# Second attention with query halves stacked on the rows and two score products a head

## The chip, the cores and the metric

The kernel runs on one core of one Trainium2 chip. The metric is the device time of one execution in microseconds (us); lower is better. TensorE (PE) multiplies matrices into eight PSUM banks, VectorE (DVE) and ScalarE (ACT) work element by element, GpSimd (POOL) does the same more slowly, and SyncE (SP) issues the transfers.

## What is computed

Two blocks of a transformer over 512 positions of 1024 features, everything in float32. The first has two layers and is not touched. The second, cut to what matters here:

```python
proj = h @ w_in                       # u_glu, q, k, v, gate_logits
u = ua * jax.nn.sigmoid(ub)
u = conv31(u) + conv_b                # depthwise, 31 taps along time
u = jax.nn.silu(layer_norm(u, conv_ln_g, conv_ln_b))
y_conv = u @ conv_w_out + conv_b_out

q1, q2, k1, k2 = rope(...)            # 8 heads of 64 each; v: 8 heads of 128
a = softmax(q1 k1^T) - lam * softmax(q2 k2^T)     # causal, in blocks of 128 queries
y_att = rms_norm(a v, head_norm) * (1 - lam_init)

g_conv, g_att = jnp.split(jax.nn.sigmoid(gate_logits), 2, axis=-1)
y = (g_conv * y_conv + g_att * y_att) @ w_o
```

A feed-forward layer follows.

## The kernel before

A float32 product is made of three fast products: each operand is split in a high and a low part, and `mm3` (lines 459 to 464) adds high x high, high x low and low x high in one bank. Weights arrive in one stream of units of 128x1024. For each unit SP loads `raw`, ACT copies the high half to `wh` (line 377), DVE subtracts to get the low half `wl` (line 380). `raw`, `wh` and `wl` are rings of three. Units that are needed for long ("held") go into 128x512 slots instead. Line 380 is the helper behind all additions, subtractions and multiplications of two tensors, line 398 the one behind scalar-tensor-tensor operations, line 377 the one behind all ACT operations, line 544 the mask with its row minimum.

The second block (`second`, line 1357) begins with the two GLU inputs (1602 to about 1711 us in the trace). Then come four parts of the attention, two heads of v each: query/key projections of four units into four banks (`pq`), copied out by ACT and rotated by `rope2`; value projections (`pv`, held units); and, as `GATES` says, some of the 16 gate units, all of them behind part 3. Then eight units of `conv_w_out_2` follow, and eight of `w_o_2` (from 2066.10 us).

Beside these projections run two lanes of generators. `beat` counts the triples of products and calls `tick` at every third; each lane then takes as many steps as its rate has saved up. The lane "conv" is the depthwise convolution: 8 tiles of 30 taps, one DVE operation each (line 398, with `cw`), in groups of three. The lane "att" is the attention: `_diff_turn` transposes the rotated queries and keys (line 1663) and splits them; `_diff_block` does the scores of one block of queries (line 1691), mask (544), exponentials on ACT, the difference (398, with `dka`), transposes (1715), product with v (1723), the normalization (`dss`, with one POOL operation) and a transpose back (1741). A score tile needs 64 rows of contraction: two softmax halves lie in rows 0 to 63 and 64 to 127 of a tile, and each half has three products.

The building program may set instructions of different lanes in another order on an engine than they are written, but each engine then runs its list strictly in that order. Banks and slots come from lists of free ones, oldest first, so a projection may be given a bank that an attention step still holds.

Of the kernel before, what the change touches and what calls it, by code (L numbers as in the profile page):

```python
# [16 lines left out]
R1, R2, R3, R4, R5, R6 = 0.9, 1.0, 0.6, 0.6, 0.8, 1.5  # L17
# [8 lines left out]
GATES = (0, 0, 0, 16)  # L26
# [56 lines left out]
def _units_second():  # L83
# [4 lines left out]
    gates = [("w_in_2", 0, 0, 8, c + 128 * m, 128) for c in (6144, 5120) for m in range(8)]  # L88
# [43 lines left out]
HELD = {i for i, u in enumerate(UNITS) if _is_held(i, u)}  # L132

# [175 lines left out]
class Net:  # L309
# [90 lines left out]
    def split(self, hi, lo, src, scale=None):  # L400
# [17 lines left out]
    def _fetch(self, between=None):  # L418
# [3 lines left out]
        off, s = PIECES[i]  # L422
        raw = self.small("raw", (128, 1024), bufs=3)
# [8 lines left out]
        if i in HELD:  # L432
            wh, wl = [], []
            per = 512 // _cols(u)
            for k in range(0, u[3], per):
# [3 lines left out]
                self.split(h, l, raw[:, c].rearrange("p (k c) -> p k c", k=n))  # L439
# [3 lines left out]
        else:  # L443
            h = self.small("wh", (128, 1024), F32R, bufs=3)
            l = self.small("wl", (128, 1024), F32R, bufs=3)
            for c in parts:
                self.split(h[:, c], l[:, c], raw[:, c])
# [909 lines left out]
    def second(self, follow, out):  # L1357
# [6 lines left out]
        def convolve(i):  # L1364
            acc = self.big(f"acc{i}")
            self.act(acc, us[i], AF.Identity, scale=self.cw[:, 31 * i + 30:31 * i + 31], bias=self.p("conv_b", i))
            for j in range(29, -1, -1):
                s = 30 - j
                self.stt(acc[:, s:], us[i][:, :512 - s], self.cw[:, 31 * i + j:31 * i + j + 1], acc[:, s:], ALU.mult, ALU.add)
                if j % 3 == 0:  # L1370
                    yield
            self.free(us[i])
            conv.append(acc)
            if i == 1:
                csum.append(self.big("csum"))
                self.add(csum[0], conv[0], conv[1])
            elif i > 1:
                self.add(csum[0], csum[0], acc)

        csum, cn = [], []  # L1380
        cl = self.lane("conv", 1, R3)
        ths = {}
# [59 lines left out]
        self.lane("conv", 1, R4)  # L1442
        for part in range(4):
            pq = [self.psum(f"pq{t}") for t in range(NTB)]
# [11 lines left out]
            self.free(pq)  # L1456
            for t in range(NTB):
                self.rope2(ra[t], cos[:, t], sin[:, t])
# [18 lines left out]
            al.waiting += self.diff_attention(part, ra, vv, ya, done)  # L1477
            if part == 3:
                cl.waiting.append(self.conv_norm(conv, csum, cn))
                self.lane("conv", 1, R5)  # L1480
            for m in range(sum(GATES[:part]), sum(GATES[:part + 1])):
# [3 lines left out]
        self.lane("att", 2, R6)  # L1485
# [155 lines left out]
    def rope2(self, a, cos, sin):  # L1641
# [9 lines left out]
        self.add(a, a, b)  # L1651
        self.free(b)

    def diff_attention(self, part, ra, vv, ya, done):
        qk = []
        left = [NTB]
        return [self._diff_turn(ra, qk)] + [self._diff_block(part, n, qk, vv, ya, left, done) for n in range(NTB)]

    def _diff_turn(self, ra, qk):
        for j in range(4):  # L1660
            pt = self.psum("qkT", (128, 4, 128))
# [168 lines left out]
```

## Time and profile before

| | |
|---|---|
| median of 3 runs | 2490.43 us (2488.10 to 2490.53) |
| the profiled execution | 2488.26 us |
| its span | 2486.1 us |
| PE busy | 2444.6 us (98%) |
| DVE busy | 1638.6 us (66%) |
| ACT busy | 1064.8 us (43%) |
| POOL busy | 318.7 us (13%) |
| mean granted clock of PE | 0.994 |

The profile is one execution, and its span begins with the first instruction; the time of the execution is 2.2 us longer than the span. Busy times of PE overlap, since a product's last columns drain while the next one starts: the distance between two starts is what a product costs in a row. The granted clock is a share of 2.4 GHz; 0.5 is 1.2 GHz.

### The profile page before, as it was taken

The numbers are of one execution on the slowest core, as the hardware profiler recorded it, in microseconds if no ns is written. First come the engines' busy times: TensorE is split into PE (matmuls) and PEld (weight loads), VectorE is DVE, ScalarE is ACT, GpSimd is POOL, SyncE is SP. The second block draws the span as 40 slices with busy tenths as digits, with TensorE's granted clock in tenths as the row PEclk, the third lists the DMA queues.
The fourth block names the chain that finished last, engine by engine and source line by source line (L and its number), as shares of the span: only waits on it lengthen the run. The fifth ranks groups of instructions, "written<-read, shape, count | busy, mean of one in ns | idle before, by whom it ended". The sixth has DMA issues, their size and how long they took to land.

```text
span 2486.1 us, 32470 instructions
## 1 busy us (share of the span) xinstructions
PE 2444.6 (98%) x12206; PEld 2053.9 (83%) x12206; DVE 1638.6 (66%) x3064; ACT 1064.8 (43%) x1984; POOL 318.7 (13%) x820
## 2 busy tenths in 40 slices
PE   9999999999999999999999999999999989999998
PEld 7888888888888888888888788988887769988887
DVE  6998755444355488865677644799899675643335
ACT  6567433332234365643423223523445565634222
POOL 7923000000056054100000000000000000000000
PEclk9999999999999999999999999999999989999999
DMA  4222232222323322133466633322211113122232
GB/s 156 86 71 77 80 132 93 96 100 94 101 97 128 97 73 75 60 102 127 133 219 207 222 113 107 126 89 103 77 60 68 47 64 119 69 93 89 94 106 76
DMA packets 83677, 256.57 MB, mean 103 GB/s; under 512 B 9536, under 2 KB 10944, under 8 KB 83520
## 3 DMA queue, kind: packets, MB, share of 16 engines
q1 hardware_dynamic: 83520, 254.50, 30.2%
q8 instruction: 95, 1.56, 0.3%
q14 instruction: 62, 0.51, 0.1%
HBM read 248.18 MB, written 6.29 MB: 102 GB/s over the span
## 4 chain that ended last, share of the span: by engine, by line
PE 83%; DVE 7%; DMA 5%; ACT 2%; issue 2%; SPq 0%; POOL 0%; DVEq 0%; POOLq 0%; ACTq 0%
PE bank L462 26%; PE bank L463 26%; PE bank L464 26%; DMA slot<-in_wada_dram 4%; DVE slot L380 2%; DVE wl L380 2%; ACT slot L377 2%; DVE slot L398 2%; PE bank L1691 1%; PE bank L1723 1%; DMA raw<-in_w_dram 0%; PE bank L1194 0%; PE bank L1206 0%; DVE slot L394 0%; PE bank L1014 0%
## 5 line engine op out<-in xcount | busy, mean ns | idle before, releaser
L462 PE MATMUL bank<-slot,wh 128*128 128x512 f32 x2456 | 964.5, 394 | 7.3 <-ACT slot L377 7.3
L464 PE MATMUL bank<-slot,wl 128*128 128x512 f32 x2456 | 959.7, 392 | 2.8 <-DVE wl L380 2.8
L463 PE MATMUL bank<-slot,wh 128*128 128x512 f32 x2456 | 959.9, 391 | 0.0
L377 ACT ACTIVATE wh<-raw 128x1024 fp32r<-128x1024 f32 (+3 forms) x369 | 385.2, 1045 | 774.2 <-PE bank L463 401.8
L380 DVE TENSOR_TENSOR wl<-raw,wh 128x1024 fp32r<-128x1024 f32 (+3 forms) x369 | 450.4, 1221 | 216.9 <-ACT wh L377 214.9
L462 PEld LDWEIGHTS bank<-slot,wh 128*128 128x128 f32 x2456 | 463.5, 189 | 105.8 <-ACT slot L377 9.1
L464 PEld LDWEIGHTS bank<-slot,wl 128*128 128x128 f32 x2456 | 462.5, 188 | 102.8 <-DVE wl L380 6.0
L463 PEld LDWEIGHTS bank<-slot,wh 128*128 128x128 f32 x2456 | 463.2, 189 | 95.3 <-DVE slot L398 0.7
L380 DVE TENSOR_TENSOR slot<-bank,slot 128x512 f32<-128x512 f32 (+4 forms) x340 | 197.4, 592 | 229.3 <-PE bank L464 207.9
L377 ACT ACTIVATE slot<-slot 128x512 fp32r<-128x512 f32 (+4 forms) x378 | 207.6, 558 | 293.6 <-DVE slot L380 269.8
L380 DVE TENSOR_TENSOR slot<-slot,slot 128x512 f32<-128x512 f32 (+4 forms) x480 | 288.4, 619 | 50.2 <-ACT slot L377 47.1
L377 ACT ACTIVATE slot<-bank 128x512 f32<-128x512 f32 (+7 forms) x398 | 182.7, 475 | 128.2 <-PE bank L464 47.8
L463 PE MATMUL bank<-wl,slot 128*128 128x512 f32 (+1 forms) x480 | 180.9, 377 | 0.0
L464 PE MATMUL bank<-wh,slot 128*128 128x512 f32 (+1 forms) x480 | 180.1, 376 | 0.0
L462 PE MATMUL bank<-wh,slot 128*128 128x512 f32 (+1 forms) x480 | 179.5, 377 | 0.0
L463 PE MATMUL bank<-slot,slot 128*128 128x256 f32 (+1 forms) x624 | 178.3, 291 | 0.3 <-DVE slot L398 0.3
L464 PE MATMUL bank<-slot,slot 128*128 128x256 f32 (+1 forms) x624 | 178.3, 290 | 0.0
L398 DVE SCALAR_TENSOR_TENSOR slot<-slot,slot 128x512 f32<-128x512 f32 (+1 forms) x184 | 123.9, 689 | 81.1 <-DMA slot<-in_wada_dram 58.0
L462 PE MATMUL bank<-slot,slot 128*128 128x256 f32 (+1 forms) x624 | 176.5, 292 | 0.3 <-ACT slot L377 0.3
L398 DVE SCALAR_TENSOR_TENSOR slot<-slot,cw,slot 128x485 f32<-128x485 f32 (+28 forms) x240 | 166.6, 731 | 1.9 <-ACT slot L377 1.1
L380 DVE TENSOR_TENSOR slot<-slot,bank 128x512 f32<-128x512 f32 (+1 forms) x104 | 66.2, 644 | 128.8 <-PE bank L464 128.5
L463 PEld LDWEIGHTS bank<-slot,slot 128*128 128x128 f32 x624 | 118.9, 192 | 2.6 <-DVE slot L398 0.5
(197 smaller groups left out, 2163.2 us busy)
## 6 DMA issues: line engine op xcount, KB each, us to landing
raw<-in_w_dram SPq DMA_DIRECT2D x373, 512.0 KB, 3.3
slot<-in_wada_dram SPq DMA_DIRECT2D x96, 256.0 KB, 5.0
raw<-in_w_dram SPq DMA_DIRECT2D x32, 448.0 KB, 3.4
slot<-in_x_dram SPq DMA_DIRECT2D x16, 256.0 KB, 3.8
xd<-slot SPq DMA_DIRECT2D x16, 256.0 KB, 3.8
slot<-xd SPq DMA_DIRECT2D x16, 256.0 KB, 3.6
out_dram<-slot SPq DMA_DIRECT2D x8, 256.0 KB, 2.0
slot<-in_bc_dram SPq DMA_DIRECT2D x8, 128.0 KB, 3.1
```

What stands on the lines that cost most here:

```text
L377: return self.nc.scalar.activation(out=out, in_=in_, func=func, scale=scale, **kw)
L380: return (eng or self.nc.vector).tensor_tensor(out=out, in0=a, in1=b, op=op)
L398: return self.nc.vector.scalar_tensor_tensor(out=out, in0=a, scalar=s, in1=b, op0=op0, op1=op1, **kw)
L462: t.matmul(ps, ah, bh, start=start, stop=False)
L463: t.matmul(ps, ah, bl, start=False, stop=False)
L464: t.matmul(ps, al, bh, start=False, stop=stop)
L1691: nc.tensor.matmul(ps[e][:, :w], qk[s][x][rows, tn], qk[2 + s][y][rows, :w], start=i == 0, stop=i == 2)
L1723: nc.tensor.matmul(po[:, e], at[e][:, b], vv[b // 2][:, b % 2, 128 * e:128 * e + 128], start=b == 0, stop=b == n)
```

## The change

The two score products. `_diff_turn` now lays the queries of one softmax half out twice on 128 rows, the high part in 64 rows and the low part in the other 64 (`qs`). Keys are copied twice side by side before their transposes (`kd`), so that a key tile has the same 64 rows twice, once as a high tile and once as a low one. One product of `qs` with the high keys and one with the low keys take the place of the three: 128 score products in place of 192. There are 32 more transposes (32 of queries and 64 of keys in place of 64). The doubling is an addition on POOL of the two rope terms, and DVE adds only the query half.

Weight halves. For the units of `w_in_2` behind the first six and for `conv_w_out_2` the low half is subtracted on POOL: 50 operations of 128x1024 and 16 of 128x512.

Gates, rates and yields. Parts 1 and 2 get two gates each and part 3 has twelve, in the order of `GATE_ORDER`. The attention lane runs at 1.65 steps a tick in place of 1.0, and the convolution lane at a rate worked out from the steps left. The accumulator of a convolution lies in a bank, and ACT copies it out at the end. `dfin` has three buffers. Some `yield`s move.

In all PE's list goes from 11,855 to 11,823 instructions, DVE's from 2,968 to 2,918, ACT's from 1,818 to 1,842 and POOL's from 825 to 907; up to the end of the GLU inputs PE's list is the same.

```diff
-R1, R2, R3, R4, R5, R6 = 0.9, 1.0, 0.6, 0.6, 0.8, 1.5
+R1, R2, R3 = 0.9, 1.65, 0.6
-GATES = (0, 0, 0, 16)
+GATES = (0, 2, 2, 12)
+GATE_ORDER = (0, 1, 2, 3, 4, 5, 8, 9, 10, 11, 12, 13, 14, 15, 6, 7)
+BESIDE = {i for i, u in enumerate(UNITS) if i >= _SECOND + GLU_HELD and u[0] in ("w_in_2", "conv_w_out_2")}
...
-            self.sub(lo, src, hi.bitcast(F32))
+            self.sub(lo, src, hi.bitcast(F32), eng)
...
+        eng = self.nc.gpsimd if i in BESIDE else None
...
-            acc = self.big(f"acc{i}")
+            acc = self.psum(f"acc{i}")
...
-            conv.append(acc)
+            conv.append(self.big(f"conv{i}"))
+            self.act(conv[i], acc)
...
+            self.free(acc)
...
+            cl.rate = steps[0] / (16 * (4 - part) + 8 / 3 * (6 - sum(GATES[:part])))
...
-            for m in range(sum(GATES[:part]), sum(GATES[:part + 1])):
+            for m in GATE_ORDER[sum(GATES[:part]):sum(GATES[:part + 1])]:
...
-        self.add(a, a, b)
+        self.add(a[:, 0:4], a[:, 0:4], b[:, 0:4])
+        k, kb = (z[:, 4:8].unsqueeze(2).to_broadcast([128, 4, 2, 64]) for z in (a, b))
+        self.add(kd, k, kb, self.nc.gpsimd)
...
+        for s in range(2):
+            pt = self.psum("qT", (128, 4, 128))
             for t in range(NTB):
+                self.nc.tensor.transpose(pt[:, t], ra[t][:, 2 * s:2 * s + 2].rearrange("p h d -> p (h d)"), self.ident)
+            src = pt.rearrange("p t d -> p (t d)")
+            qs = [self.big("qs", F32R) for _ in range(2)]
+            for e in range(2):
+                rows, rest = slice(64 * e, 64 * e + 64), slice(64 - 64 * e, 128 - 64 * e)
+                self.act(qs[e][rows], src[rows])
+                self.sub(qs[e][rest], src[rows], qs[e][rows].bitcast(F32))
             self.free(pt)
+            ks = []
+            for e in range(2):
+                yield
+                pt = self.psum("kT", (128, 4, 128))
+                for t in range(NTB):
+                    self.nc.tensor.transpose(pt[:, t], kd[t][:, 2 * s + e].rearrange("p i d -> p (i d)"), self.ident)
+                ks.append((self.big("kh", F32R), self.big("kl", F32R)))
+                self.split(*ks[e], pt.rearrange("p t d -> p (t d)"))
+                self.free(pt)
...
-            for i, (x, y) in enumerate(((0, 0), (0, 1), (1, 0))):
-                for e in range(2):
-                    rows = slice(64 * e, 64 * e + 64)
-                    nc.tensor.matmul(ps[e][:, :w], qk[s][x][rows, tn], qk[2 + s][y][rows, :w], start=i == 0, stop=i == 2)
+            for e in range(2):
+                for i in range(2):
+                    nc.tensor.matmul(ps[e][:, :w], qk[s][0][e][:, tn], qk[s][1][e][i][:, :w], start=i == 0, stop=i == 1)
...
+        self.lanes["conv"].rate = 0.7
```

The order on the engines, at the end of part 1's query/key projections. First PE before: L462 to L464 are the three products of `mm3`, L1691 the scores of one half.

```order
L462 MATMUL bank_64<-wh_152,slot_12627 128x512
L463 MATMUL bank_64<-wl_155,slot_12627 128x512
L464 MATMUL bank_64<-wh_152,slot_12628 128x512
L1691 MATMUL bank_70<-slot_13899,slot_13838 128x512
L1691 MATMUL bank_70<-slot_13900,slot_13838 128x512
L1691 MATMUL bank_70<-slot_13899,slot_13839 128x512
L462 MATMUL bank_63<-slot_14379,slot_12564 128x256
L463 MATMUL bank_63<-slot_14380,slot_12564 128x256
L464 MATMUL bank_63<-slot_14379,slot_12565 128x256
```

Three products of a score stand between the last triple of the query/key projections and the first of the value projections (128x256).

The same place on PE after: the last 13 instructions of a stretch of 28 that has no projection, and the gate's projection that ends it. L1720 is the new score product, L1744 the transposes of the difference, L1752 the product with v, L1770 the transpose back, L469 and L470 the new lines of `mm3`; x2 stands for two that read alike.

```order
L1720 MATMUL bank_63<-slot_13887,slot_13857 128x512
L1720 MATMUL bank_68<-slot_13964,slot_13911 128x512
L1720 MATMUL bank_68<-slot_13965,slot_13911 128x512
L1744 MATMUL bank_64<-cst,slot_14038 128x128 x2
L1770 MATMUL bank_66<-cst,slot_14197 128x128 x2
L1720 MATMUL bank_69<-slot_13944,slot_13910 128x384
L1720 MATMUL bank_69<-slot_13945,slot_13910 128x384
L1744 MATMUL bank_70<-cst,slot_14040 128x128 x2
L1752 MATMUL bank_64<-slot_13786,slot_14108 128x128 x2
L469 MATMUL bank_63<-slot_12564,wh_152 128x512
L470 MATMUL bank_63<-slot_12565,wh_152 128x512
```

The projection that follows writes bank_63, in which a score of 512 columns has just been put; it can start when the mask has read that.

DVE after, at the end of the 53 instructions that stand beside this stretch: L404 with `cw` is a tap of the convolution (now into bank_67), L404 with `dka` the difference of the two halves, L551 the mask and its row minimum.

```order
L404 SCALAR_TENSOR_TENSOR bank_67<-slot_13234,cw_11510,bank_67 128x489
L404 SCALAR_TENSOR_TENSOR dka_14035<-dsm_14033,nlam_11506,dri_14034 128x2
L400 TENSOR_SCALAR drs_14037<-dri_14034 128x2
L404 SCALAR_TENSOR_TENSOR bank_67<-slot_13234,cw_11510,bank_67 128x488
L386 TENSOR_TENSOR dss_13971<-dss_13971,dfin_14126 128x2
L404 SCALAR_TENSOR_TENSOR slot_14038<-slot_14039,dka_14035,slot_14038 128x256
L404 SCALAR_TENSOR_TENSOR slot_14040<-slot_14041,dka_14035,slot_14040 128x256
L404 SCALAR_TENSOR_TENSOR bank_67<-slot_13234,cw_11510,bank_67 128x487
L551 ISA slot_14310,dmx_14043<-bank_63,slot_13534 128x512
L551 ISA dmx_14043 128x1
```

The mask that reads bank_63 is the last but one of the list; ahead of it stand taps, rope operations and the differences. At the ends of parts 2 and 3 PE's list has the like, with 33 and 25 instructions, ended by the value projections.

## Rows read from the trace of the kernel before

**Rows 1.** The page, part 1: busy time, share of span, instructions.
```profile
PE 2444.6 (98%) x12206; PEld 2053.9 (83%) x12206; DVE 1638.6 (66%) x3064; ACT 1064.8 (43%) x1984; POOL 318.7 (13%) x820
```
**Rows 2.** Windows: length, busy of PE, PEld, DVE, ACT, POOL; PE's clock; DMA.
```profile
1800.00:1820.00 20.00, 19.38 (x125) 17.16 (x125) 18.42 (x37) 8.16 (x20) 0.00 (x0) 1.00 0.04 15
...
1920.00:1940.00 20.00, 17.33 (x79) 12.84 (x77) 17.73 (x42) 9.29 (x26) 0.00 (x0) 0.91 0.16 53
...
1980.00:2000.00 20.00, 12.06 (x74) 9.07 (x72) 16.24 (x38) 17.38 (x41) 2.37 (x3) 0.83 0.01 2
2000.00:2020.00 20.00, 19.35 (x72) 15.17 (x73) 15.00 (x33) 11.33 (x28) 0.00 (x0) 0.83 0.37 128
...
2060.00:2080.00 20.00, 18.60 (x148) 17.40 (x147) 11.67 (x26) 12.90 (x33) 1.39 (x2) 1.00 0.32 114
```
**Rows 3.** Windows around the two dips of the granted clock.
```profile
1931.70:1935.10 3.40, 3.40 (x10) 2.63 (x9) 3.40 (x13) 1.70 (x6) 0.00 (x0) 0.50 0.00 0
1993.10:2006.80 13.70, 9.50 (x29) 7.20 (x30) 13.70 (x33) 13.70 (x32) 0.00 (x0) 0.50 0.06 16
```
**Rows 4.** Timeline of PE: start, length, instruction, [idle before <-releaser].
```profile
1989.40 0.60 PE L1663 MATMUL bank<-cst,slot 128*128 128x128 f32 x4
1989.96 0.33 PE L1691 MATMUL bank<-slot,slot 64*128 64x128 f32 x2
...
1994.64 0.90 PE L1691 MATMUL bank<-slot,slot 64*128 64x128 f32 x5 [2.74 <-DVE slot L380]
...
2000.65 0.80 PE L462 MATMUL bank<-slot,wh 128*128 128x512 f32 x1 [0.97 <-ACT slot L377]
```
**Rows 5.** Timeline of PE, two runs of score products and what follows them.
```profile
1837.12 0.94 PE L1691 MATMUL bank<-slot,slot 64*128 64x128 f32 x12
1837.99 0.38 PE L462 MATMUL bank<-slot,slot 128*128 128x256 f32 x1
...
1869.61 0.96 PE L1691 MATMUL bank<-slot,slot 64*128 64x512 f32 x3
1870.50 0.50 PE L462 MATMUL bank<-slot,wh 128*128 128x512 f32 x1
1870.84 0.40 PE L463 MATMUL bank<-slot,wh 128*128 128x512 f32 x1
1871.08 0.40 PE L464 MATMUL bank<-slot,wl 128*128 128x512 f32 x1
```
**Rows 6.** Groups of DVE, 1720 to 2070 us: busy us, mean ns | idle before.
```profile
L380 DVE TENSOR_TENSOR wl<-raw,wh 128x1024 fp32r<-128x1024 f32 x33 | 40.3, 1221 | 11.7 <-ACT wh L377 11.1 <-PE bank L464 0.6
L380 DVE TENSOR_TENSOR slot<-slot,slot 128x512 f32<-128x512 f32 x57 | 37.9, 687 | 0.3 <-ACT slot L377 0.2
...
L398 DVE SCALAR_TENSOR_TENSOR slot<-slot,slot,slot 128x512 f32<-128x512 f32 x16 | 11.4, 746 | 4.1 <-DMA slot<-xd 4.0
L544 DVE CUSTOM_DVE_ANT_0 slot<-bank,slot 128x512 f32<-128x512 f32 x16 | 10.9, 688 | 8.1 <-PE bank L1691 8.1
...
L380 DVE TENSOR_TENSOR slot<-slot,slot 128x256 f32<-128x256 f32 x24 | 9.2, 421 | 0.2 <-ACT slot L377 0.2
```
**Rows 7.** Groups of POOL over the whole span: busy us, mean ns | idle before.
```profile
L380 POOL TENSOR_TENSOR s_xx<-slot,s_steps 128x256 f32<-128x256 f32 x32 | 19.1, 618 | 0.5
...
L380 POOL TENSOR_TENSOR s_xx<-slot,s_steps 128x64 f32<-128x64 f32 x32 | 10.7, 354 | 0.5
```
**Rows 8.** Timeline of DVE and POOL in the first block.
```profile
916.88 0.73 POOL L380 TENSOR_TENSOR slot<-s_xx 128x256 f32<-128x256 f32 x1
916.89 0.74 DVE L380 TENSOR_TENSOR sm<-sm,es 128x4 f32<-128x4 f32 x1
...
917.67 0.48 DVE L544 CUSTOM_DVE_ANT_0 slot<-bank,cst,nsink 128x256 f32<-128x256 f32 x1
917.69 0.61 POOL L380 TENSOR_TENSOR s_xx<-slot,s_steps 128x256 f32<-128x256 f32 x1
```
**Rows 9.** Timeline of DVE: six operations in a row.
```profile
1988.59 4.06 DVE L398 SCALAR_TENSOR_TENSOR slot<-slot,slot,slot 128x512 f32<-128x512 f32 x6
```

More of the change, by code (lines that the diff above doesn't have):

```diff
@@ L87, in _units_second @@
         u.append(("w_in_2", 0, 0, 8, 128 * i, 128))
-    gates = [("w_in_2", 0, 0, 8, c + 128 * m, 128) for c in (6144, 5120) for m in range(8)]
+    gates = [("w_in_2", 0, 0, 8, (6144 if m < 8 else 5120) + 128 * (m % 8), 128) for m in GATE_ORDER]
     for part in range(4):
@@ L1456, in second @@
             self.free(pq)
+            kd = [self.big("kd", shape=(128, 4, 2, 64)) for _ in range(NTB)]
             for t in range(NTB):
-                self.rope2(ra[t], cos[:, t], sin[:, t])
+                self.rope2(ra[t], kd[t], cos[:, t], sin[:, t])
             wv = [self.unit("w_in_2") for _ in range(2)]
@@ L1476, in second @@
                 ya[m] = self.big(f"ya{m}")
-            al.waiting += self.diff_attention(part, ra, vv, ya, done)
+            al.waiting += self.diff_attention(part, ra, kd, vv, ya, done)
             if part == 3:
                 cl.waiting.append(self.conv_norm(conv, csum, cn))
-                self.lane("conv", 1, R5)
-            for m in range(sum(GATES[:part]), sum(GATES[:part + 1])):
+                cl.rate = steps[0] / 5
+            for m in GATE_ORDER[sum(GATES[:part]):sum(GATES[:part + 1])]:
                 gate(m)
@@ L1484, in second @@
         self.finish("conv")
-        self.lane("att", 2, R6)
         ys = []
@@ L1650, in rope2, with diff_attention, _diff_turn @@
         self.mul(a, a, tab(cos))
[L1651 removed]
+        self.add(a[:, 0:4], a[:, 0:4], b[:, 0:4])
+        k, kb = (z[:, 4:8].unsqueeze(2).to_broadcast([128, 4, 2, 64]) for z in (a, b))
+        self.add(kd, k, kb, self.nc.gpsimd)
         self.free(b)
[L1654 removed]
+    def diff_attention(self, part, ra, kd, vv, ya, done):
         qk = []
         left = [NTB]
[L1657 to L1661, printed above, removed]
+        return [self._diff_turn(ra, kd, qk)] + [self._diff_block(part, n, qk, vv, ya, left, done) for n in range(NTB)]
+    def _diff_turn(self, ra, kd, qk):
+        for s in range(2):
+            pt = self.psum("qT", (128, 4, 128))
             for t in range(NTB):
[L1663 to L1669 removed]
+                self.nc.tensor.transpose(pt[:, t], ra[t][:, 2 * s:2 * s + 2].rearrange("p h d -> p (h d)"), self.ident)
[5 more added lines that the diff above has]
+                self.sub(qs[e][rest], src[rows], qs[e][rows].bitcast(F32))
+            self.free(pt)
+            ks = []
[7 more added lines that the diff above has]
+                self.free(pt)
+            qk.append((qs, ks))
+            if s == 1:
+                self.free(ra, kd)
             yield
@@ L1673, in _diff_block @@
         nc = self.nc
-        while len(qk) < 4:
+        while len(qk) < 2:
             yield
@@ L1709, in _diff_block @@
         if n == NTB - 1:
-            self.free(qk)
+            self.free([[q, k] for q, k in qk])
         at = []
@@ L1726, in _diff_block @@
             self.free(at[e])
-            if e == 0:
-                yield
-        fin = self.small("dfin", (128, 2), bufs=2)
+        yield
+        fin = self.small("dfin", (128, 2), bufs=3)
         self.stt(fin, ss, HEAD_LIMIT, rs, ALU.is_lt, ALU.mult)
@@ L1732, in _diff_block @@
         self.powm(ss, ss, 2)
+        yield
         self.mul(ss, ss, fin)
```

22 lines of the change are left out of this document (9 added, 13 removed).

## The prediction, before the run

> **What bounds the kernel now.** I read the page first: TensorE (PE) is busy 98% of the span [rows 1], so the time is PE's own work plus the places where PE waits or runs at half clock. Next the windows of 20 us over the second attention: PE is full in nearly all of them. The idle time stands in five (20 less PE's busy time): 0.62 + 2.67 + 7.94 + 0.65 + 1.40 = 13.3 us [rows 2]. VectorE (DVE) is at 16 to 18 of 20 us in the first three of these. Two narrower windows show the granted clock at 0.50, that is 1.2 GHz, each behind a stretch in which PE waited [rows 3]. The first costs half of 3.4 us, 1.7. In the second PE has no projection until 2000.65 [rows 4]; from there to 2006.80 it loses half of 6.15, 3.1. So waits and clock take 13.3 + 4.8 = 18.1 us: all that a smoother second attention can give back.
>
> The largest of these stretches is the pattern to remember. From 1989.96 to 2000.65 PE's list holds score products alone, with no projection behind which a wait could hide, and it sits through 2.74 us waits for DVE [rows 4]. DVE meanwhile runs one queue of long vector operations.
>
> **The change part by part.**
>
> *Score products.* Before, each of the two softmax halves of a head has three products on 64 rows. Most of the time one half stands alone between projections: three of 512 columns take 1870.50 - 1869.61 = 0.89 us, and the first projection behind them 0.34 where the next takes 0.24, so 0.10 more [rows 5]. Twelve of 128 columns take 0.87, so three take 0.22 [rows 5]. I draw a line between these for 256 and 384 columns (0.44 and 0.67). Sixteen triples of each width are 16 x (0.22 + 0.44 + 0.67 + 0.89) = 35.5 us, and 52 separate runs, counted in the same view, pay the 0.10: 40.7 in all. After, there are 32 products of each width on 128 rows. One of 512 columns is priced as a projection of that size, 0.24; in proportion 0.18 and 0.12, and 0.11 for 128 columns: 32 x 0.65 = 20.8. That saves 19.9. The stacking adds 32 transposes; four take 1989.96 - 1989.40 = 0.56 [rows 4], so 32 x 0.14 = 4.5. Net on PE: -15.4. PE is the bound, so this is on the path.
>
> A rule speaks against this part. The Trainium skill ("TensorEngine Tiling (Array Packing)", Overview) says that products with a contraction of 64 rows can run side by side, up to twice as fast. If all pairs had, the old triples would have cost 17.8 + 5.2 = 23.0, and the gain would be 2.2 in place of 19.9. The rows bear this out only where both halves stand next to each other, as in the twelve of 0.87; a half that stands alone takes 0.30 for each product of 512 columns, more than the 0.24 of a full-height one.
>
> *Weight halves to GpSimd (POOL).* DVE loses subtractions of 1.22 us, 33 of them in 350 us [rows 6], so 40 us of about 300 busy ones. POOL gets them. A POOL operation of 64 columns takes 354 ns and of 256 columns 618 [rows 7], a slope of 1.38 ns a column: 1024 columns cost at least 0.62 + 768 x 0.00138 = 1.67 us. From a 256-column operation of 0.73 us [rows 8], four times that is 2.9. I take 2.2, and keep both ends. A unit of eight blocks is 24 projections of 0.24, so 5.8 us on PE; even 2.9 fits inside this, with two more units ready in the ring. Price on PE as long as DVE and POOL don't block each other: 0.
>
> *Doubled keys.* Half of the rope addition leaves DVE (512 columns at 687 ns become 256 at 421 [rows 6], 16 x 0.27 = 4.3 us less) and POOL gets 16 additions of 512 columns, at 0.97 to 1.46 by the same two rows; I take 1.2. Queued behind them on POOL are the next weight halves.
>
> *DVE and POOL together.* Here the trace warns. A DVE multiplication of 4 columns, both inputs in SBUF, took 0.74 us, exactly as long as the 256-column POOL operation that ran beside it. The next DVE operation, which reads a PSUM bank, took 0.48 us beside another POOL operation of 0.61, and did not last as long as that one [rows 8]. So each POOL operation can hold back a DVE operation with two SBUF inputs. The Trainium skill ("SBUF — State Buffer", Who interferes with whom) states just this, an exclusive lock; by it the convolution's accumulator, now in a bank, keeps its taps out of the lock, but the rope operations stay in it.
>
> *Accumulator in PSUM.* The taps are the same in number; a tap's price with a bank on both sides is not in the trace. The nearest rows are the mask operation from a bank, 688 ns, and the operation with three SBUF inputs, 746 [rows 6]: between -0.06 and +0.06 us each, off PE's path between the stretches below. One of the eight banks is now held for each convolution, and that is the price that I look for in the order.
>
> *Gates, rates, yields.* Four gates move from behind the last part into parts 1 and 2: PE's work is the same, it is cover that moves. The first block's PE list does not change, so nothing moves before about 1602 us.
>
> *What the order then shows.* At the end of the query/key projections of parts 1, 2 and 3 PE's new list has a stretch with attention alone: 28, 33 and 25 instructions, ended by a projection that needs a bank which the attention still holds (the section on the change shows the first). Before, the value projections followed at once. In these stretches DVE's list holds 53, 51 and 36 instructions, and the last mask that frees the bank stands at its end: PE must sit DVE's list out. I price it with DVE's rows: 421 ns at 256 columns and 687 at 512 [rows 6] give 0.155 us + 1.04 ns a column. Six operations with a mean of 746 ns took 4.06 us end to end [rows 6, 9], not 4.48, so each hides 0.084. First stretch: 18 of 256 columns, 6 of 512, 8 taps of about 490, 2 of 384, 2 of 128, 9 small ones and 8 accumulator reads, which go into the 0.084: 16.4 us. In the same way 15.6 and 12.3. Together 44.3, of which PE's own work covers 14.0 (28, 33 and 25 instructions at 0.11 to 0.24) and DVE has done about 4 when PE arrives (its first rope operations can start once the first bank is copied). Left: 26.3 us of waits as the **lower bound** without any lock. POOL has in these stretches 1 + 3 + 3 weight halves and 4 + 4 + 2 key additions: 7 x 2.2 + 10 x 1.2 = 27.4 us. If DVE stood still for all of it: 53.7, the **upper bound**. By my sums about half of DVE's time there goes to operations that touch a bank and so escape; I take 40% of 27.4, 11, and so 37.
>
> *Clock.* Each stretch looks like that of 1989.96 to 2000.65, so I expect half clock behind it: 1.7 to 3.1 each, 5.1 to 9.3 for three; I take 8.
>
> **Sum**, against the profiled execution, 2488.3 (2.1 below the median of the runs shown, 2490.4): 2488.3 - 15.4 - 18.1 (all old waits and dips gone, the kindest case) + 37 + 8 = 2499.8. I say 2500.
>
> **The rivals.**
>
> *A, the forecast:* three stretches, lock in part: 2491 to 2511.
>
> *B, on the other side: the stretches are light.* With 40 us less on DVE's list it is ahead when PE comes, and each stretch costs only what the lighter one of before did, 2.67 idle and 1.7 clock [rows 2, 3]. 2488.3 - 15.4 - 18.1 + 3 x 4.4 = 2468 (2458 to 2480), faster. For it: DVE has slack between the stretches. Against it: most of the DVE instructions there depend on the copies of the banks just finished, so a free DVE can't do them early. It decides where the three cost less than 31 us with the clock (2454.8 + 31 = 2485.8).
>
> *C, no lock, short dips:* 2454.8 + 26.3 + 5.1 = 2486 (2481 to 2491), on the edge of faster. For it: POOL's operations are few, and half of DVE's touch a bank.
>
> *D, full lock:* 2454.8 + 53.7 + 9.3 = 2518 (2511 to 2528). For it: the 0.74 us row; each key addition becomes ready at the same moment as DVE's own half of the same addition, so they collide every time.
>
> *E, the score change gives nothing,* because the halves did run side by side: 2500 + 17.7 = 2518. This is the rule of the skill's page on array packing; the rows for a half alone speak against it.
>
> **How the numbers follow.** A 0.43, B 0.17, C 0.16, D 0.18, E 0.06. The likeliest is A, so 2500. A measurement of this kernel can tell about 0.2%, 5 us, from no change: faster is below 2485.5, slower above 2495.4. Faster: B and half of C, 0.25. Same: the other half of C and the lower end of A, 0.18. Slower: the rest, 0.57. A alone reaches from 2491 to 2511. The range for 8 in 10 takes in C, the upper half of B and most of D and E: 2470 to 2524; it leaves out the lower half of B and the ends of D and E.
>
> **What would show it.** In the profile after: the score products with 128 rows at about 0.24 us for 512 columns and no slow first projection (gain right), or 0.30 and more (wrong). Three gaps in the PE windows, each 7 to 16 us, at the ends of the query/key projections, PE waiting there for a mask or a DVE multiplication, and a clock of 0.5 behind each (A); gaps under 4 us (B). DVE operations with two SBUF inputs beside a POOL operation at far more than 421 or 687 ns (A, D), or unchanged (C). Weight halves on POOL at 1.7 to 2.9 us. The forecast is wrong if PE doesn't stop at these three places, or if it waits for POOL's weight halves in the projections, which I price at 0.

## The result

The changed kernel takes 2516.14 us (median, 2511.77 to 2516.57) against 2489.26 before: a ratio of 1.0104 (95% interval 1.0091 to 1.0116), 27 us slower. I had forecast slower, by 10. The profile of the changed kernel, the page's busy times:

```profile
PE 2438.8 (97%) x12174; PEld 2064.0 (82%) x12174; DVE 1646.2 (65%) x3014; ACT 1078.7 (43%) x2008; POOL 480.5 (19%) x902
```

Set against [rows 1]: PE is busy for 6 us less, though more of that time is now at half clock. POOL has 162 us more. DVE, which gave away 66 subtractions, is no less busy than before, 1646 us against 1639. That is the line to stop at: 50 x 1.22 + 16 x 0.69 = 72 us were taken off DVE, and its busy time did not fall.

Two windows, from the end of part 0's projections to the last gates and to `conv_w_out_2`. The columns are length, busy us of PE, PEld, DVE, ACT and POOL, the granted clock of PE, and the transfers. The kernel before:

```profile
1740.00:1940.00 200.00, 196.44 (x1071) 160.09 (x1070) 178.16 (x379) 94.06 (x232) 7.80 (x8) 0.99 0.18 64
1940.00:2100.00 160.00, 149.95 (x823) 121.46 (x821) 104.03 (x233) 97.61 (x238) 7.24 (x10) 0.96 0.25 86
```

The changed one:

```profile
1740.00:1940.00 200.00, 163.53 (x896) 139.28 (x895) 175.89 (x371) 101.42 (x263) 70.60 (x45) 0.86 0.17 58
1940.00:2100.00 160.00, 150.81 (x769) 126.26 (x767) 118.52 (x212) 91.61 (x199) 47.19 (x24) 0.97 0.27 89
```

PE is idle for 36.5 us in the first window, in place of 3.6, at a clock of 0.86. In the second it is idle for 9.2, in place of 10.1. PE's waits from 1740 to 1940 us, the columns being total, times and longest:

```profile
PE bank L1744 <- DVE slot L404: 24.7, 5, 9.4
PE bank L1720 <- DVE dmx L551: 8.9, 3, 6.8
```

L1744 transposes the difference of the two halves, L404 makes it, L551 is the mask: PE waits for DVE, at the ends of parts 1 to 3, as was foreseen. It waits inside the stretches, for the difference above all, and not at the projection that ends them. The first stretch on PE (start, length, [idle <-releaser]):

```profile
1755.06 0.86 PE L1720 MATMUL bank<-slot,slot 128*128 128x384 f32 x4
1760.49 0.74 PE L1744 MATMUL bank<-cst,slot 128*128 128x128 f32 x2 [4.56 <-DVE slot L404]
...
1774.01 0.77 PE L469 MATMUL bank<-slot,wh 128*128 128x512 f32 x1
1774.58 0.63 PE L470 MATMUL bank<-slot,wh 128*128 128x512 f32 x1
1775.01 0.63 PE L471 MATMUL bank<-slot,wl 128*128 128x512 f32 x1
```

The projections behind it start 0.57 and 0.43 us apart in place of 0.24, about half speed. What DVE and POOL did in that wait of 4.56 us:

```profile
1757.25 2.92 DVE L386 TENSOR_TENSOR slot<-slot,slot 128x256 f32<-128x256 f32 x3
1760.10 0.60 DVE L404 SCALAR_TENSOR_TENSOR slot<-slot,dka,slot 128x128 f32<-128x128 f32 x2
```
```profile
1756.88 2.34 POOL L386 TENSOR_TENSOR wl<-raw,wh 128x1024 fp32r<-128x1024 f32 x1 [0.48 <-ACT wh L383]
```

Three rope operations with two SBUF inputs take 2.92 us; they end only after POOL's weight half has. The groups of DVE (busy us, mean ns) and POOL show the same over the whole attention. DVE from 1720 to 2100 us, to be read against 421 ns in [rows 6] for the same shape:

```profile
L386 DVE TENSOR_TENSOR slot<-slot,slot 128x256 f32<-128x256 f32 x42 | 37.9, 936 | 4.0 <-ACT slot L383 3.9
```

POOL from 1600 to 2150:

```profile
L386 POOL TENSOR_TENSOR wl<-raw,wh 128x1024 fp32r<-128x1024 f32 x50 | 121.9, 2441 | 185.5 <-ACT wh L383 179.6 <-issue 3.4 <-PE bank L1680 2.6
L386 POOL TENSOR_TENSOR slot<-slot,slot 128x512 f32<-128x512 f32 x16 | 22.1, 1385 | 27.3 <-DVE slot L386 22.3 <-DVE dka L404 2.4 <-DVE dfin L404 1.9
```

I set every DVE operation from 1600 to 2150 us against the median of its shape in the kernel before and added up what was more than 0.1 us above: 56.3 us in the changed kernel, 0.0 in the one before. So of the 72 us taken off DVE, 56 came back as waiting for POOL: 14.3 us of them before 1740, 20.6 from there to 1940 and 21.4 behind it. Another 11 us are new work of the score part, which makes 16 subtractions more than before. Sixteen now have 64 rows in place of 128 and are no shorter for it (0.69 us, as for 128 rows in [rows 6]):

```profile
L386 DVE TENSOR_TENSOR slot<-bank,slot 64x512 fp32r<-64x512 f32 x16 | 11.0, 689 | 5.8 <-ACT slot L383 5.5
```

### The profile page after: what moved, and what is told of

Read it like the earlier page. It is cut to its first block, busy times and chain, and to the rows that moved or that the text cites. A ratio compares the mean times of both kernels' runs of the same rounds, so it can differ in the third digit from the quotient of the medians.

```text
span 2514.8 us, 32513 instructions
## 1 busy us (share of the span) xinstructions
PE 2438.8 (97%) x12174; PEld 2064.0 (82%) x12174; DVE 1646.2 (65%) x3014; ACT 1078.7 (43%) x2008; POOL 480.5 (19%) x902
## 4 chain that ended last, share of the span: by engine, by line
PE 76%; DVE 12%; DMA 6%; ACT 3%; issue 2%; POOL 1%; SPq 1%; DVEq 0%; POOLq 0%; ACTq 0%
PE bank L469 24%; PE bank L470 24%; PE bank L471 23%; DVE slot L386 5%; DMA slot<-in_wada_dram 4%; DVE wl L386 2%; ACT slot L383 2%; DVE slot L404 2%; DMA raw<-in_w_dram 2%; DVE bank L404 1%; POOL wl L386 1%; PE bank L1752 1%; ACT wh L383 0%; DVE slot L400 0%; PE bank L1201 0%
## 5 line engine op out<-in xcount | busy, mean ns | idle before, releaser
L469 PE MATMUL bank<-slot,wh 128*128 128x512 f32 x2456 | 965.4, 394 | 6.0 <-ACT slot L383 5.9
L470 PE MATMUL bank<-slot,wh 128*128 128x512 f32 x2456 | 961.1, 392 | 2.9 <-DVE slot L404 2.9
L469 PEld LDWEIGHTS bank<-slot,wh 128*128 128x128 f32 x2456 | 464.1, 189 | 100.9 <-ACT slot L383 5.9
L470 PEld LDWEIGHTS bank<-slot,wh 128*128 128x128 f32 x2456 | 464.0, 189 | 97.7 <-DVE slot L404 3.6
L386 DVE TENSOR_TENSOR wl<-raw,wh 128x1024 fp32r<-128x1024 f32 (+3 forms) x319 | 389.8, 1222 | 204.8 <-ACT wh L383 203.3
L386 DVE TENSOR_TENSOR slot<-bank,slot 128x512 f32<-128x512 f32 (+4 forms) x356 | 208.7, 596 | 237.0 <-PE bank L471 209.1
L386 DVE TENSOR_TENSOR slot<-slot,slot 128x512 f32<-128x512 f32 (+4 forms) x473 | 305.0, 664 | 65.0 <-ACT slot L383 61.5
L383 ACT ACTIVATE slot<-bank 128x512 f32<-128x512 f32 (+8 forms) x422 | 195.9, 479 | 124.3 <-PE bank L471 38.9
L404 DVE SCALAR_TENSOR_TENSOR slot<-slot,slot 128x512 f32<-128x512 f32 (+1 forms) x184 | 131.9, 732 | 88.5 <-DMA slot<-in_wada_dram 60.2
L469 PE MATMUL bank<-slot,slot 128*128 128x256 f32 (+1 forms) x624 | 179.0, 294 | 2.4 <-ACT slot L383 2.4
L471 PE MATMUL bank<-slot,slot 128*128 128x256 f32 (+1 forms) x624 | 180.9, 292 | 0.0
L404 DVE SCALAR_TENSOR_TENSOR bank<-slot,cw,bank 128x493 f32<-128x493 f32 (+14 forms) x240 | 174.4, 735 | 9.6 <-ACT bank L383 5.7
L470 PE MATMUL bank<-wl,slot 128*128 128x512 f32 (+1 forms) x480 | 180.5, 376 | 0.1
L470 PE MATMUL bank<-slot,slot 128*128 128x256 f32 (+1 forms) x624 | 180.0, 292 | 0.3 <-DVE slot L404 0.3
L469 PE MATMUL bank<-wh,slot 128*128 128x512 f32 (+1 forms) x480 | 179.7, 378 | 0.1
L386 POOL TENSOR_TENSOR wl<-raw,wh 128x1024 fp32r<-128x1024 f32 x50 | 121.9, 2441 | 185.5 <-ACT wh L383 179.6
```

The source lines that it names most:

```text
L383: return self.nc.scalar.activation(out=out, in_=in_, func=func, scale=scale, **kw)
L386: return (eng or self.nc.vector).tensor_tensor(out=out, in0=a, in1=b, op=op)
L404: return self.nc.vector.scalar_tensor_tensor(out=out, in0=a, scalar=s, in1=b, op0=op0, op1=op1, **kw)
L469: t.matmul(ps, ah, bh, start=start, stop=False)
L470: t.matmul(ps, ah, bl, start=False, stop=False)
L471: t.matmul(ps, al, bh, start=False, stop=stop)
```

## The experiments

The theories: **lock** (POOL's operations that read SBUF hold up DVE's with two SBUF inputs), **rate** (the attention lane at 1.65 makes lumps in PE's list), **bank** (the projection behind a stretch waits for a bank of the attention, and the accumulator took one), and **list** (whatever the cause, DVE's in-order list is what PE sits out). Times are medians; the kernel before took 2488 to 2491 beside them.

### The lock

Weight halves back on DVE:

```diff
-        eng = self.nc.gpsimd if i in BESIDE else None
+        eng = None
```

> The changed kernel with one part undone: the low halves of the weights are subtracted on VectorE again. Lock theory (GpSimd's long operations hold VectorE's operations with two SBUF inputs, and that makes the three stretches long): those VectorE operations fall back to about 421 ns (256 columns) and 687 ns (512), the three stretches lose 10 us and more, and the time falls from 2516 to 2495-2505. Rate theory (the attention lane at 1.65 steps a tick puts attention steps in a lump for which VectorE's list is too long, whoever subtracts): the stretches stay, VectorE has 66 more operations in its list, and the time stays at 2510-2525.

2503.21 us, 13 faster than the changed kernel, although DVE had 72 us more to do. The stretched time fell from 56.3 to 12.0 us; what is left belongs to the key additions, for in a run below without these and without POOL's subtractions it is 1.0. But the three stretches did not lose the 10 us that I expected. PE waits as long in them as before, and the idle time that went away lies behind part 3:

```profile
1740.00:1940.00 200.00, 160.21 (x896) 137.21 (x894) 188.26 (x408) 100.91 (x266) 23.64 (x22) 0.88 0.15 53
1940.00:2100.00 160.00, 157.41 (x861) 134.73 (x860) 118.30 (x227) 98.13 (x213) 6.10 (x7) 1.00 0.31 102
```

PE idles 39.8 us at the part ends, where it had 36.5, and 2.6 behind them, where it had 9.2. The run can't say what the lock costs by itself, since it moved work as well. The next one comes closer: POOL writes zeros in place of the low halves, which the products then lack, and reads nothing for them.

```diff
-            self.sub(lo, src, hi.bitcast(F32), eng)
+            (self.sub(lo, src, hi.bitcast(F32)) if eng is None else eng.memset(lo.bitcast(F32), 0.0))
```

> The changed kernel; GpSimd fills the 66 low weight halves with zeros in place of subtracting, so it writes them but reads nothing (the low part of these weights is left out of the products). TensorE's and VectorE's lists are nearly those of the changed kernel, and VectorE has no more work than there. Lock theory: of 56 us by which VectorE's operations were stretched beside GpSimd, about 12 stay (the key additions), and with the three stretches 10-15 us shorter the time falls to 2495-2506. If the lists alone (not the lock) make the waits: within 6 us of 2516.

2492.26 us, ratio 1.0008 (0.9999 to 1.0018): **24 of the 27 us are gone**, a little more than the lock theory gave. The stretched time is 11.6 us. A rope operation on DVE that lies wholly beside a memset on POOL, in this run:

```profile
1827.85 0.42 DVE L386 TENSOR_TENSOR slot<-slot,slot 128x256 f32<-128x256 f32 x1
```
```profile
1827.68 0.95 POOL L409 MEMSET wl<- 128x1024 f32 x1 [5.20 <-PE bank L470]
```

0.42 us, the price of the shape without POOL. A memset is also shorter (0.95 us against 2.44) and does not wait for ACT's high half, so a part of the 24 may be POOL being done sooner. Nor are the lists quite the same: the first two stretches are as long in both traces (PE idles 18.9 us in them in place of 25.8), but from about 1880 us PE's order is another, and the third stretch is cut in two. The windows of this run:

```profile
1740.00:1940.00 200.00, 171.25 (x962) 147.65 (x960) 175.28 (x397) 105.02 (x271) 42.41 (x45) 0.89 0.17 56
1940.00:2100.00 160.00, 157.55 (x859) 134.51 (x858) 95.47 (x200) 97.55 (x214) 21.42 (x24) 1.00 0.31 103
```

PE's idle time falls by 7.7 us at the part ends (36.5 to 28.8) and by 6.7 behind part 3 (9.2 to 2.5), and the clock there is back at 1.00. The lock was not confined to the three stretches. The changed kernel's own trace shows it behind part 3, in PE's two longest waits there and in what DVE and POOL did before them:

```profile
1990.05 0.73 PE L1744 MATMUL bank<-cst,slot 128*128 128x128 f32 x2 [2.33 <-DVE slot L404]
1987.56 2.43 DVE L404 SCALAR_TENSOR_TENSOR slot<-slot,dka,slot 128x128 f32<-128x128 f32 x1
1987.46 2.39 POOL L386 TENSOR_TENSOR wl<-raw,wh 128x1024 fp32r<-128x1024 f32 x1 [5.20 <-ACT wh L383]
```
```profile
2051.55 0.50 PE L470 MATMUL bank<-slot,wh 128*128 128x512 f32 x1 [2.86 <-DVE slot L404]
2044.62 2.89 DVE L404 SCALAR_TENSOR_TENSOR slot<-slot,slot 128x512 fp32r<-128x512 f32 x1
2047.44 2.85 DVE L404 SCALAR_TENSOR_TENSOR slot<-slot,slot,slot 128x512 f32<-128x512 f32 x1
2044.40 5.34 POOL L386 TENSOR_TENSOR wl<-raw,wh 128x1024 fp32r<-128x1024 f32 x2 [2.65 <-ACT wh L383]
```

The first DVE operation takes 0.35 us elsewhere, the two others 0.69 and 0.75.

Two more pairs say the same: rate 1.3 with POOL subtracting 2519.49, with the memset 2486.99 (33 us); old scores 2519.20 and 2496.20 (23 us). These runs stand below.

The accumulator back in SBUF, where each tap has two SBUF inputs:

```diff
-            acc = self.psum(f"acc{i}")
+            acc = self.big(f"acc{i}")
...
-            conv.append(self.big(f"conv{i}"))
-            self.act(conv[i], acc)
+            conv.append(acc)
...
-            self.free(acc)
```

> The changed kernel with one part undone: the convolution's accumulator lies in SBUF again, so its 240 taps have two SBUF inputs each, beside the same operations of GpSimd. Lock theory: the taps are now held as well, VectorE's operations are stretched by 80-120 us in all in place of 56, and the time goes up to 2530-2560, as in the run with the other bank order (2565), of which this is one half. Bank theory (the bank that the accumulator takes makes the stretches): with the bank back the waits fall, 2495-2510.

2563.67 us (two executions), 48 slower, just above the lock theory's range, and the stretched time is 107.6 us. But the price is not all lock. One of PE's waits is 22.6 us for a rope operation, and what stands in DVE's list there is this, with POOL idle beside it:

```profile
1726.17 12.84 DVE L404 SCALAR_TENSOR_TENSOR slot<-slot,cw,slot 128x482 f32<-128x482 f32 x20
```

Twenty taps in a row at 0.64 us each, undisturbed: the list was built in another order. The rest of that wait is the lock again: when POOL starts, four rope operations take 5.96 us. How much of the 48 us is lock and how much is list stays open. The bank theory, which had this run faster, is out as the main cause.

### Rate, banks, taps

```diff
-R1, R2, R3 = 0.9, 1.65, 0.6
+R1, R2, R3 = 0.9, 1.3, 0.6
```

> The changed kernel with one number changed: the attention lane at 1.3 steps a tick in place of 1.65. Rate theory: the longest stretches of TensorE's list without a projection shrink from 28, 33 and 21 instructions to 12, 24 and 19, the waits there fall from about 44 us to 20-25, and the time falls to 2485-2500. Lock theory: GpSimd's work is the same and so are its collisions with VectorE; the time stays within 8 us of 2516.

2519.49 us: no gain, and the stretched time is 66.2 us. With POOL reading, the rate theory failed here: the waits moved (one of 7.4 us before the transposes of the queries, one of 5.2 before the value projections) and kept their sum. Without the lock the same number does a little:

> The changed kernel with GpSimd writing zeros for the low weight halves (they are left out; no reads, as in the run at 2492) and the attention lane at 1.3 in place of 1.65. If the rate makes what waits are left at the part ends (45 us in the memset run): 2470-2485. If they belong to the burst of rope and mask operations at a part's end, at either rate: within 6 us of 2492.

2486.99 us, 5 below the memset run at 1.65, inside the second reading's 6 us. The 45 us that I named as left in the memset run are not in its trace: it is 28.8 at the part ends and 2.5 behind. Of the 28.8 the rate does take 10 (18.6 are left), and behind part 3 it gives 3 back (5.3). That the rest belongs to the burst of rope and mask operations is not shown.

The same number on the kernel before, 1.0 to 1.65:

> The kernel before with one number changed: its attention lane at 1.65 steps a tick in place of 1.0. Rate theory: stretches of 19, 45 and 35 instructions without a projection appear in TensorE's list at the ends of parts 1 to 3, and the time goes up by 15-35 us to 2505-2525, though no weight half is on GpSimd. Lock theory: no collisions, so within 6 us of 2489.

2522.56 us, 32 slower without any lock. So lumps are dear where DVE carries everything, though not where I expected all of them: 18.7 us of idle stand at the part ends, and 12.5 in one wait for ACT behind part 3, where the convolution's normalization came too late.

Bank order (accumulator in SBUF as above, and the banks of the query/key projections first in the list):

```diff
             self.free(pq)
+            self.free_banks[:] = self.free_banks[-4:] + self.free_banks[:-4]
```

> The changed kernel with the accumulator back in SBUF, and the four banks of the query/key projections given out first when they come free, so that the value projections get a bank which only ScalarE's copy still holds. The stretches at the ends of parts 1 and 3 vanish from TensorE's list (28, 33, 21 become 0, 24, 0; a new one of 32 stands further back). Bank theory (the projection behind a stretch waits for a bank of the attention): the waits fall by 15-25 us, time 2490-2503. If VectorE is late in any case, the waits turn up elsewhere: within 8 us of 2516.

2564.55 us, the same as with the accumulator in SBUF alone (2563.67). The order of the banks gave nothing; the stretches vanished from PE's list where I had said, and the waits stood elsewhere.

Ten taps of 30:

```diff
-            for j in range(29, -1, -1):
+            for j in range(9, -1, -1):
```

> The changed kernel with 10 of the 30 taps of each convolution (20 are left out): VectorE has 160 operations of about 0.73 us less, 117 us. If VectorE's list is what TensorE sits out at the part ends, the waits there fall from 44 us to under 20 and the time to 2465-2490. If the waits come from the chain of one attention step (mask, exponentials, difference, transposes), whatever else VectorE has to do: 2505-2516.

2509.09 us (two executions): DVE lost 160 operations, the kernel only 7 us. Idle from 1740 to 1940 us fell from 36.5 to 23.8, but behind part 3 it rose from 9.2 to 13.6. At the part ends the 20 taps were about a third of the wait; that the rest is the chain with its rope operations is argued, not shown. The time lies in the second reading's range: fewer taps alone don't free PE.

### The gates

All gates behind part 3 again, with the memset:

```diff
-GATES = (0, 2, 2, 12)
-GATE_ORDER = (0, 1, 2, 3, 4, 5, 8, 9, 10, 11, 12, 13, 14, 15, 6, 7)
+GATES = (0, 0, 0, 16)
+GATE_ORDER = tuple(range(16))
```

> The changed kernel with GpSimd writing zeros for the low weight halves (left out), and all 16 gates behind part 3 as before. If the gates spread over parts 1 and 2 give cover there: slower than the memset run (2492) by 5-20 us, with longer waits at the ends of parts 2 and 3 (stretches of 36 and 41 instructions in TensorE's list in place of 33 and 18). If they give none: within 5 us of 2492.

2529.80 us, 38 slower than the memset run, twice what I gave. With a lane at 1.65 and without POOL's reads the spread gates are worth 38 us of cover. I had put their price at nothing.

### The scores

Old scores in the changed kernel (three products of 64 rows, no doubled keys):

```diff
-            for e in range(2):
-                for i in range(2):
-                    nc.tensor.matmul(ps[e][:, :w], qk[s][0][e][:, tn], qk[s][1][e][i][:, :w], start=i == 0, stop=i == 1)
+            for i, (x, y) in enumerate(((0, 0), (0, 1), (1, 0))):
+                for e in range(2):
+                    rows = slice(64 * e, 64 * e + 64)
+                    nc.tensor.matmul(ps[e][:, :w], qk[s][x][rows, tn], qk[2 + s][y][rows, :w], start=i == 0, stop=i == 2)
```

> The changed kernel with the score part undone: three products of 64 rows for each half, no doubled keys, no key additions on GpSimd. If the stacked scores give what was worked out (15 us net on TensorE), this is 10-20 us slower than the changed kernel, 2526-2536. If they give nothing on the path, it is within 6 us of 2516. If the key additions on GpSimd cost more than the scores give, it is faster, 2500-2510.

> The changed kernel with GpSimd writing zeros (low weight halves left out) and the old scores, so no doubled keys and no operation of GpSimd that reads SBUF beside the small ones. If the stacked scores are worth their 15 us on the path where the lists are those of the changed kernel: 2502-2510, against 2492 with them. If the waits take the gain: 2486-2496.

2519.20 and, without the lock, 2496.20 us: the stacked scores are worth 3 and 4 us there, not 15 (and 3 is within the spread of the two kernels' executions). PE's work did change by that much: its busy time is 20.1 us longer with the old scores (2458.9 against 2438.8), and 13.3 without the lock (2447.5 against 2434.2). But PE's idle time from 1740 to 2100 is shorter by nearly as much: 26.5 us in place of 45.7, and 18.9 in place of 31.2.

The score part alone on the kernel before; the keys are doubled by ACT in place of `kd`:

```diff
+                self.act(kh[rows], src[rows])
+                self.act(kh[rest], src[rows])
+                self.sub(kl[rows], src[rows], kh[rows].bitcast(F32))
+                self.act(kl[rest], kl[rows].bitcast(F32))
```

> The kernel before with the score part alone: stacked queries, two products a head, old gates, rates and weight halves; the keys are doubled by two more ScalarE copies a tile in place of GpSimd's additions, so there are no more transposes than before. TensorE has 15.4 + 4.5 = about 20 us less to do by the working of the prediction, 13 by the difference that the old scores made in the changed kernel. If the score part pays where the lists around it stay as they were: 2470-2482. If a shorter TensorE list only waits longer for VectorE: 2484-2495.

2488.64 us, ratio 0.9998 (0.9988 to 1.0007): nothing. PE's busy time did fall, by 14.9 us to 2429.7; its waits rose by as much. Its windows:

```profile
1740.00:1940.00 200.00, 186.54 (x1041) 161.10 (x1040) 188.97 (x389) 114.66 (x266) 7.75 (x8) 0.98 0.20 68
1940.00:2100.00 160.00, 142.72 (x793) 122.17 (x792) 113.61 (x248) 106.35 (x252) 7.57 (x10) 0.93 0.25 86
```

13.5 us of idle in place of 3.6, then 17.3 in place of 10.1. DVE is at 189 of 200, where it had 178: it has the 16 further subtractions here too, 11 us, so it is nearly full just where PE has less to do. But ACT also has more to do, 115 us in place of 94, with the doubled copies, and of PE's named waits in the first window 6.7 us are put down to DVE and 6.9 to ACT. That DVE alone bounds this stretch is not shown.

The attention lane at 1.1, with the score part and without it:

```diff
-R1, R2, R3, R4, R5, R6 = 0.9, 1.0, 0.6, 0.6, 0.8, 1.5
+R1, R2, R3, R4, R5, R6 = 0.9, 1.1, 0.6, 0.6, 0.8, 1.5
```

> The kernel before with the score part alone (2489 at rate 1.0) and the attention lane at 1.1. Its waits at rate 1.0 stand behind part 3, about 21 us from 1980 to 2010, where a stretch of 59 instructions is left over; at 1.1 that becomes 31. If a slightly faster lane takes attention out of that end without a lump at the part ends: 2475-2484, faster than both kernels. If any faster lane makes lumps at the part ends (rate 1.65 cost the kernel before 32 us): 2490-2500.

> The kernel before with the attention lane at 1.1 and nothing else. If the 8 us of the run with the score part at 1.1 belong to the rate: 2478-2484. If to the scores (with the rate only as cover): 2487-2500.

With the scores **2480.73 us, ratio 0.9974 (0.9964 to 0.9983), faster than both kernels**. Without them 2488.81, ratio 0.9995 (0.9985 to 1.0004), no change. So the gain belongs to the scores, with the rate as its condition: 8 us by the medians, 5 by the two ratios. Idle behind part 3 is 14.3 us in the first:

```profile
1940.00:2100.00 160.00, 145.73 (x856) 127.10 (x856) 117.77 (x256) 104.76 (x242) 7.48 (x8) 0.96 0.24 83
```

The gates of the changed kernel on top, at 1.1 and at 1.3:

```diff
-GATES = (0, 0, 0, 16)
+GATES = (0, 2, 2, 12)
+GATE_ORDER = (0, 1, 2, 3, 4, 5, 8, 9, 10, 11, 12, 13, 14, 15, 6, 7)
```

> The kernel before with the score part, the attention lane at 1.1 and the gates spread over the parts as in the changed kernel (2, 2, 12); weight halves on VectorE, accumulator in SBUF. Without the gates this is 2481. If four gates of cover between the parts are worth something here too: 2468-2477. If the waits at rate 1.1 stand elsewhere (13.5 us from 1980 to 2000, behind part 3, where cover is now taken away): 2481-2490.

> The same with the attention lane at 1.3, so that less attention is left behind part 3 (the longest stretch there is 25 instructions in place of 35). If spread gates give cover for a faster lane: 2465-2477, the fastest yet. If a faster lane makes waits at the part ends with the gates as well: 2482-2500.

2488.71 and 2508.95 us, both worse than 2480.73. At 1.3 PE idles 25.2 us from 1940 to 2100 in place of 14.3, so cover is missing behind part 3. At 1.1 the trace doesn't show where the 8 us lie: the two windows have 28.7 us of idle in place of 27.1, and the execution that was profiled is the longest of ten (2497.56), with a wait of 10.5 us in the first block, which the edit does not touch. So the same four gates that save 38 us for a lane at 1.65 cost some here; why they do at 1.1 stays open.

## Why the forecast was right in direction and too small

- **The three stretches: right in place, releaser and size.** The sum had 37 us of waits; PE idles 36.5 from 1740 to 1940. Both halves of the 37 came out: 26.3 without the lock against 28.8 in the memset run (where the key additions still read), and 11 for the lock against 7.7.
- **"All old waits and dips gone, the kindest case", 18.1 us: this step failed.** I called it kind and still put nothing against it in the forecast's own value. From 1940 to 2100 PE idles 9.2 us at a clock of 0.97, where it had 10.1 at 0.96. These are other waits than before, but as many us, and with the half clock (the last two lines below) about 13 of the 18.1 us were there again: 9.2, and half of the 8.1 us that PE was busy at 0.50. The sum with 13 us more is 2513. By these runs the lock made most of this: its lines behind part 3 stand above, and without POOL's subtractions the idle time there is 2.5 or 2.6 us at 1.00. I had looked for the lock in the three stretches only, because that is where I had counted POOL's operations; 21 of the 56 us by which DVE was stretched lie behind them.

```profile
1759.32:1776.38 17.06, 11.40 (x34) 8.37 (x35) 16.99 (x49) 9.31 (x32) 4.83 (x4) 0.50 0.10 32
1834.41:1858.30 23.89, 9.94 (x36) 7.67 (x37) 23.78 (x57) 9.46 (x33) 8.15 (x6) 0.50 0.11 38
1919.74:1933.40 13.66, 6.82 (x24) 5.10 (x25) 13.66 (x33) 6.28 (x18) 7.19 (x5) 0.50 0.21 77
1988.01:1994.84 6.83, 4.68 (x12) 3.60 (x13) 5.64 (x12) 2.46 (x9) 1.84 (x1) 0.50 0.23 77
2052.86:2056.28 3.42, 3.42 (x10) 2.68 (x9) 1.32 (x2) 2.15 (x4) 1.24 (x1) 0.50 0.10 37
```

- **The clock, 8 us: right in place, its size not settled.** The first three lines are the half clock at the three stretches, 54.6 us, most of it inside the stretch and not behind it. Counted as in the prediction, by the projections behind the stretch alone, it costs 3 us; half of all that PE was busy in these lines is 14. The rest of the miss, some 4 us, may lie here.
- **The lock: the mechanism was right, the term mis-sized.** 11 us in the sum, for the stretches alone; 24 is what went away with POOL's reads. This is the same miss as the 13 us, seen from the other side, and not to be added to it. That the full lock of the stretches, 27.4 us, is close to 24 is chance. Rival D (2511 to 2528) had the time, 2516, which lies outside A (2491 to 2511); but D had it by a price for the stretches that they did not reach: 53.7 us, where 36.5 were idle. So D's number came out by luck.
- **"PE is the bound, so this is on the path": failed.** The 15.4 us of the scores were right as work of PE (13 to 20 in the runs), and 0 to 8 of them reached the end. The sum had priced the score part on PE alone. DVE was at 16 to 18 of 20 us in [rows 2], and the part gave it 11 us more. The scores alone gave nothing clear of the noise at rate 1.0, 3 and 4 us in the changed kernel with and without the lock, 5 to 8 at rate 1.1. It is not what made the sum miss, since the waits had a term of their own there.
- **Gates at nothing.** They are worth 38 us with the lane at 1.65. No term of the sum is off by this, for the stretches were priced from lists that had the gates in place; but the text had them as neutral, and they are not.
- **Rivals.** B is out: the stretches are not light. C, no lock, is out as the kernel stands; the memset run is nearly that kernel (the key additions still read) and took 2492 where C gave 2486. E, that halves ran side by side, is out: by it PE would have gained 2.2 us and paid 4.5 for the transposes, and its busy time fell by 13 to 20. A pair of score products of 384 columns now takes 1778.54 - 1778.18 = 0.36 us in the trace, the 0.18 each of the sum:

```profile
1778.18 0.51 PE L1720 MATMUL bank<-slot,slot 128*128 128x384 f32 x2
1778.54 0.40 PE L470 MATMUL bank<-slot,wh 128*128 128x512 f32 x1
```

- **POOL's prices** were at the upper half of the range: 2.44 us for 1024 columns (1.67 to 2.9, taken 2.2), 1.39 for 512 (0.97 to 1.46, taken 1.2). PE did not wait for POOL's weight halves in the projections; it waited once, 0.5 us, for a key addition. A tap into a bank takes 729 ns at 490 columns where it took 723: nothing, as put down.

What stays open: in the memset run 28.8 us of idle are left at the part ends, with no one cause shown. The slower rate takes 10 of them, and 5 us of the time; the gates already save 38; in the changed kernel 20 taps of 30 make about a third of the waits.

## What to carry to other kernels

Work that is moved to GpSimd is not free for VectorE: before moving it, list which VectorE operations have two SBUF inputs and stand beside it, and count all of them, not only those on a path that you have found. Price a part on every engine that it touches: here the saving of the scores was worked out for TensorE alone, and little of it reached the end, with VectorE at 16 to 18 of 20 us. Where the next engine is that full, try the saving alone before adding the parts that are to make room for it. Here the smallest version, scores alone with a slightly faster lane, was the only one clearly faster than the kernel before.

## What the runs showed of the hardware

The block goes by reads, not by POOL being busy: beside a `memset` of 128x1024 a 256-column operation with two SBUF inputs took its 0.42 us, beside a subtraction of the same shape three of them took 2.92, and over the whole block 45 us of DVE's stretched time went away when POOL wrote the low halves without reading. This bears out the Trainium skill ("SBUF — State Buffer", Who interferes with whom), which says that such operations contend with a GpSimd instruction that reads SBUF and not with one that only writes it. The smallest operations suffer as much as large ones. In the changed kernel, before the third stretch's longest wait (9.4 us), a DVE operation of 128x2 took 2.29 us, in place of 0.16, beside a weight half on POOL:

```profile
1922.15 2.29 DVE L404 SCALAR_TENSOR_TENSOR dfin<-dss,drs 128x2 f32<-128x2 f32 x1
```
```profile
1921.90 2.52 POOL L386 TENSOR_TENSOR wl<-raw,wh 128x1024 fp32r<-128x1024 f32 x1
```

Two input tensors in SBUF are not the only mark. Three tensor-scalar operations of 128x128, with one tensor from SBUF and one value for each row, took 2.42 to 2.46 us beside a weight half in place of 0.28; they are 6.5 of the 56.3 us. One of them:

```profile
1613.95 2.42 DVE L400 TENSOR_SCALAR slot<-cst,rstd 128x128 f32<-128x128 f32 x1 [0.18 <-POOL rstd L600]
1613.88 2.40 POOL L386 TENSOR_TENSOR wl<-raw,wh 128x1024 fp32r<-128x1024 f32 x1
```
